# First layer of a diffusion block: modulation piece turned before the first inverse rms, which stays in PSUM

## The chip, the cores and the metric

The kernel runs on one core of a Trainium2 chip. The metric is the device time of one launch in microseconds (us), the median of three runs. TensorE (PE) multiplies, VectorE (DVE) and ScalarE (ACT) do elementwise work, GpSimd (POOL) and SyncE (SP) are used here for transfers and small work.

## The reference, cut to what matters

Two layers act on 512 latent and 256 context tokens of width 1024. Only the beginning of layer 0 is touched:

```
m = silu(cond) @ w_mod + b_mod                 # shift, scale, gate ... per condition (c and c_ctx)
h = rmsnorm(x, norm_mix) * (1 + scale) + shift # latent tokens with c, context tokens with c_ctx
p = h @ w_in                                   # 2560 columns, 20 tiles of 128
```

So the first product needs the inverse rms of every token, and for each 128 channels the shift and scale of those channels.

## The kernel before, in words

Activations lie transposed: eight tiles `x[k]` of 128 channels x 776 columns (512 latent tokens, 8 columns of gap, 256 context tokens). Every product runs as three fp32r matmuls (L185 low weight x high input, L186 high weight x low input, L187 high x high), since each number is split into a high part (an ACT cast) and a low part (a DVE subtraction), for weights in `weights` and `split` (L164 to L175). A matmul covers 512 latent or 256 context columns.

`start` (L424 to L458) computes, in the order of the code:

- the sum of squares `ss` (ACT squares, DVE adds);
- piece 0 of the modulation: `mod_piece` (L227) loads four quarters of 512 KB (tile `wmod`), multiplies them with `csil` (32 matmuls, seen as 64 rows each of matmul and weight load, L238) into an accumulator in the PSUM slot `ms`, copies it to SBUF (ACT, L243), transposes it on PE (L244), copies that (ACT, L246) and adds the bias (DVE, L247); `make_gain` (L278) then gives the gain for two of the eight channel tiles. Piece q serves channel tiles 2q and 2q+1;
- the inverse rms in `rstd` (L316): means on PE (L303), Newton steps on six numbers per partition (DVE), a diagonal `rd` (DVE, L325), and two matmuls with ones (L335) that spread it over all partitions into a PSUM slot; ACT copies it to the SBUF tile `r` (L444);
- high and low parts of the first three weight tiles of `w_in`;
- piece 1, then for each pair of channel tiles `mod_in` (L343): `xr = x * r` (DVE, L348), gain and shift (ACT L357 with DVE L358 for tiles 0 and 1, ACT L360 for the others), cast and low part; then the products of these two channel tiles with the three weight tiles into the slots `sl[0]` to `sl[2]`. Pieces 2 and 3 are traced right after the products of tiles 0 and 1.

After that `layer0_input` (L461) gates slots 0 and 1 (`glu`: ACT L573, DVE L582) and goes on with the fourth weight tile, which needs slot 0 again.

PSUM: there are four `slot` tiles of 128 x 1024 fp32. Slot `ms` holds the accumulator in columns 0:128 and the transposed piece in 768:896. The inverse rms goes to columns 0:512 and 520:776 of `sl[0]`.

Order: the framework takes instructions in the order in which the Python code traces them, finds what must wait for what in that order, and puts in the waits. Within this it fills each engine's queue by a simulated timeline, so independent instructions may be issued in another order than traced. `issue_after(i)` adds one edge: what the block traces on the engine of `i` is queued behind `i`. Nothing in it waits for another engine. Transfers of this stage all go through SP's queue, in traced order, 16 quarters of `wmod` with 14 buffers.

Of the kernel before, what the change touches and what calls it, by code (L numbers as in the profile page):

```python
# [12 lines left out]
F32 = mybir.dt.float32  # L13
BF16 = mybir.dt.bfloat16
F32R = mybir.dt.float32r
I32 = mybir.dt.int32
AF = mybir.ActivationFunctionType
ALU = mybir.AluOpType
PSUM = bass.MemoryType.PSUM

P = 128
DM = 1024
KT = DM // P
# [4 lines left out]
T = C0 + CTX  # L28
# [36 lines left out]
class Kern:  # L65
# [98 lines left out]
    def split(self, src, hi, lo):  # L164

        self.act_mark = self.nc.scalar.copy(hi, src)  # L166
        self.mark = self.nc.vector.tensor_tensor(lo, src, hi.bitcast(F32), op=ALU.subtract)  # L167

    def weights(self, dram, n=1024, into=None):
# [54 lines left out]
                    self.nc.tensor.matmul(s[:, lo:hi], wh, xl, start=False, stop=k == len(rhs) - 1)  # L224


    def mod_piece(self, l, lo, hi, at, dram, acc, tr, room):  # L227

        nc = self.nc
        for quarter in range(4):  # L230
            if quarter == 2:
                yield
            w = room(quarter)
            nc.sync.dma_start(w, dram[quarter])
            for kk in range(2):
                k = quarter * 2 + kk
                for j in range(4):
                    nc.tensor.matmul(  # L238
                        acc[32 * j:32 * j + 2, :], self.csil[:, k, :], w[:, kk, j * P:(j + 1) * P],
                        start=k == 0, stop=k == KT - 1,  # L240
                    )
        sb = self.tmp.tile([P, P], F32, name="modsb", tag="r", bufs=1)
        nc.scalar.copy(sb, acc)  # L243
        nc.tensor.transpose(tr, sb, self.ident)  # L244
        sb = self.tmp.tile([P, P], F32, name="modsb", tag="r", bufs=1)
        nc.scalar.copy(sb, tr)  # L246
        nc.vector.tensor_tensor(  # L247
            self.mod[:, l, lo:hi, :].rearrange("p (a b) c -> p a b c", a=2)[:, :, at:at + 2, :],
            sb.rearrange("p (a b c) -> p a b c", a=2, b=2)[:, :, :, 0:2],
            self.p("bmod")[:, l * 48 + lo:l * 48 + hi].rearrange("p (a b) -> p a b", a=2)[:, :, at:at + 2]  # L250
            .unsqueeze(3).broadcast_to([P, 2, 2, 2]), op=ALU.add)
        yield
# [60 lines left out]
            eng.tensor_tensor(y, t, y, op=ALU.mult)  # L313
        return y

    def rstd(self, ss, segs, ones2, slot, eng=None, pool=None, project=None):  # L316

        nc = self.nc
        chunks = [c for lo, hi in segs for c in range(lo, hi, P)]
        n = len(chunks)  # L320
        o = slot
        off = segs[0][0] - segs[0][0] % C0
        y = self.inverse(ss, chunks, ones2, o[:, segs[0][0] - off:segs[0][0] - off + 2 * n], eng or nc.gpsimd)
        d = (pool or self.tmp).tile([P, n, P], F32, name="rd", tag="rd", bufs=1)
        nc.vector.tensor_tensor(  # L325
            d, self.ident.unsqueeze(1).broadcast_to([P, n, P]), y.unsqueeze(2).broadcast_to([P, n, P]), op=ALU.mult
        )
        if project:
            with self.tc.issue_after(self.stats.ins):
                next(project)  # L330
        i = 0
        with self.tc.issue_after(self.product.ins) if project else nullcontext():
            for lo, hi in segs:
                m = (hi - lo) // P
                nc.tensor.matmul(  # L335
                    o[:, lo - off:hi - off], self.onesm, d[:, i:i + m, :].rearrange("p n c -> p (n c)"), start=True, stop=True)
                i += m
        return o[:, segs[0][0] - off:segs[-1][1] - off]
# [4 lines left out]
    def mod_in(self, h, k, r, n, l, shift, segs, raw=None):  # L343

        nc = self.nc
# [13 lines left out]
            else:  # L359
                nc.scalar.activation(t[:, s0:s1], xr[:, s0:s1], AF.Identity, scale=gain, bias=add)  # L360
        if k < 2:
            nc.vector.tensor_tensor(h[k][1][:, lo:hi], t[:, lo:hi], h[k][0][:, lo:hi].bitcast(F32), op=ALU.subtract)  # L362
        else:
            self.split(t[:, lo:hi], h[k][0][:, lo:hi], h[k][1][:, lo:hi])

# [58 lines left out]
    def start(self, ph):  # L424
# [5 lines left out]
            self.square_in(k, 0, T)  # L430
        sl = [self.slot() for _ in range(3)]
        ms = self.slot()
        nc.vector.memset(ms[:, 0:P], 0.0)

        def piece(q):
            room = lambda _: ph.tile([P, 2, 512], F32, name="wmod", tag="wmod", bufs=14)
            for _ in self.mod_piece(0, 0, 16, 2 * q, a["wm0"][q], ms[:, 0:P], ms[:, 768:768 + P], room):
                pass
            self.make_gain(0, 0, 1, self.p("nmix")[:, 0:8], 2 * q, 2 * q + 2)

        piece(0)
        rp = self.rstd(self.ss, segs, self.ones2, sl[0], eng=nc.vector, pool=ph)
        r = self.tmp.tile([P, T], F32, name="r", tag="ss", bufs=1)
        nc.scalar.copy(r, rp)  # L444
        room = [[ph.tile([P, DM], F32R, name=t) for t in ("whi0", "wlo0")], None, None]
        first = [self.weights(a["w_in"][m], into=room[m]) for m in range(3)]
        piece(1)
        h = self.new_h()
        for q in range(4):
            for k in (2 * q, 2 * q + 1):  # L450
                self.mod_in(h, k, r, 0, 0, 0, segs)
            for k in (2 * q, 2 * q + 1):
                for s, w in zip(sl, first):
                    self.wide_gemm(s, w, h, segs, [k])
            if q == 0:
                piece(2)
                piece(3)
        return h, sl  # L458


# [793 lines left out]
```

## Time and profile before

| what | value |
|---|---|
| median of 3 runs | 1461.02 us (1460.01 to 1461.03) |
| the profiled execution | 1462.82 us, its span 1461.0 us |
| busy: PE, PE weight loads, DVE, ACT, POOL | 97%, 85%, 74%, 44%, 12% of the span |
| granted TensorE clock over the span | 0.997 |
| HBM traffic | 172 GB/s over the span |

Busy shares are means over stages with different limits. [...] An fp32 matmul has two rows, an fp32r one has one. "Idle before" an instruction is named after what ended it.

### The profile page before, as it was taken

The numbers are of one execution on the slowest core, as the hardware profiler recorded it, in microseconds if no ns is written. First come the engines' busy times: TensorE is split into PE (matmuls) and PEld (weight loads), VectorE is DVE, ScalarE is ACT, GpSimd is POOL, SyncE is SP. The second block draws the span as 40 slices with busy tenths as digits, with TensorE's granted clock in tenths as the row PEclk, the third lists the DMA queues.
The fourth block names the chain that finished last, engine by engine and source line by source line (L and its number), as shares of the span: only waits on it lengthen the run. The fifth ranks groups of instructions, "written<-read, shape, count | busy, mean of one in ns | idle before, by whom it ended". The sixth has DMA issues, their size and how long they took to land.

```text
span 1461.0 us, 24131 instructions
## 1 busy us (share of the span) xinstructions
PE 1421.9 (97%) x9470; PEld 1249.1 (85%) x9470; DVE 1083.3 (74%) x1750; ACT 649.8 (44%) x1105; POOL 181.3 (12%) x427
## 2 busy tenths in 40 slices
PE   5999999999999999999999999999999999999997
PEld 3888888888888888888888878867799999999897
DVE  6699998689878557565534679787767977777676
ACT  5422224473223223123213365687765745545455
POOL 0000001112222212112212110243200000000000
PEclk9999999999999999999999999999999999999999
DMA  9325433036787767847725315264532444444441
GB/s 375 113 71 174 159 116 130 30 101 204 212 223 190 218 194 197 250 156 185 162 98 100 111 59 159 67 134 110 122 116 97 157 152 158 146 156 157 148 130 68
DMA packets 80546, 215.69 MB, mean 148 GB/s; under 512 B 10032, under 2 KB 10160, under 8 KB 80304
## 3 DMA queue, kind: packets, MB, share of 16 engines
q1 hardware_dynamic: 63408, 174.29, 36.1%
q0 software_dynamic: 17024, 39.86, 13.0%
q8 instruction: 74, 1.21, 0.3%
q14 instruction: 40, 0.33, 0.1%
HBM read 209.39 MB, written 41.94 MB: 172 GB/s over the span
## 4 chain that ended last, share of the span: by engine, by line
PE 82%; DVE 7%; DMA 5%; ACT 3%; issue 2%; POOL 1%; SPq 0%; DVEq 0%; ACTq 0%
PE slot L185 20%; PE slot L186 20%; PE slot L187 19%; DMA wraw<-in_w_down 3%; PE av L1091 2%; DVE wlo L167 2%; PE pt L1081 2%; PE s L1062 2%; PE av L185 2%; PE av L186 2%; PE av L187 1%; ACT whi L166 1%; PE slot L220 1%; PE slot L224 1%; PE slot L221 1%
## 5 line engine op out<-in xcount | busy, mean ns | idle before, releaser
L185 PE MATMUL slot<-h,wlo 128*128 128x256 f32 (+1 forms) x1152 | 382.5, 334 | 2.8 <-DVE ub L582 1.2
L186 PE MATMUL slot<-h,whi 128*128 128x256 f32 (+1 forms) x1152 | 382.5, 333 | 0.2 <-DVE h L362 0.2
L187 PE MATMUL slot<-h,whi 128*128 128x256 f32 (+1 forms) x1152 | 382.7, 332 | 0.0
L166 ACT CAST whi<-wraw 128x1024 fp32r<-128x1024 f32 (+2 forms) x249 | 219.9, 892 | 240.8 <-PE slot L187 88.1
L167 DVE TENSOR_TENSOR wlo<-wraw,whi 128x1024 fp32r<-128x1024 f32 (+2 forms) x249 | 254.4, 1027 | 72.2 <-ACT whi L166 71.5
L185 PEld LDWEIGHTS slot<-h,wlo 128*128 128x128 f32 x1152 | 216.5, 188 | 29.0 <-issue 2.0
L186 PEld LDWEIGHTS slot<-h,whi 128*128 128x128 f32 x1152 | 217.0, 188 | 23.1 <-DVE h L362 0.5
L187 PEld LDWEIGHTS slot<-h,whi 128*128 128x128 f32 x1152 | 217.0, 188 | 21.8
L382 DVE SCALAR_TENSOR_TENSOR cf<-slot,par,cf 128x775 f32<-128x775 f32 (+1 forms) x92 | 92.6, 1009 | 97.8 <-ACT cf L380 97.7
L185 PE MATMUL slot<-gh,wlo 128*128 128x512 f32 (+1 forms) x435 | 148.8, 344 | 2.1 <-ACT gh L166 1.1
L186 PE MATMUL slot<-gl,whi 128*128 128x512 f32 (+1 forms) x435 | 147.9, 341 | 0.0
L187 PE MATMUL slot<-gh,whi 128*128 128x512 f32 (+1 forms) x435 | 147.6, 340 | 0.0
L380 ACT ACTIVATE cf<-slot,par 128x776 f32<-128x776 f32 (+1 forms) x46 | 41.4, 901 | 192.8 <-PE slot L187 188.7
L590 DVE SCALAR_TENSOR_TENSOR cacc<-ub,par,cacc 128x783 f32<-128x783 f32 x120 | 118.4, 1035 | 0.3
L266 DVE CUSTOM_DVE_ANT_0 junk<-wmod,cb 128x1024 bf16<-128x1024 f32 x80 | 97.5, 1218 | 22.1 <-DMA wmod<-in_wmt 20.5
L372 DVE SCALAR_TENSOR_TENSOR x<-slot,mod,x 128x256 f32<-128x256 f32 (+1 forms) x139 | 80.9, 612 | 40.9 <-PE slot L187 40.4
L185 PEld LDWEIGHTS slot<-gh,wlo 128*128 128x128 f32 x435 | 81.4, 188 | 12.7 <-ACT gh L166 1.3
L187 PEld LDWEIGHTS slot<-gh,whi 128*128 128x128 f32 x435 | 81.8, 188 | 9.8
L186 PEld LDWEIGHTS slot<-gl,whi 128*128 128x128 f32 x435 | 81.9, 188 | 9.6 <-DVE mod L247 0.2
L1069 DVE CUSTOM_DVE_ANT_0 sm<-s,mask,nsink 128x640 f32<-128x640 f32 (+1 forms) x58 | 46.6, 819 | 13.9 <-PE pt L1081 10.7
L860 ACT ACTIVATE sgf<-cf 128x776 f32<-128x776 f32 (+1 forms) x44 | 32.6, 742 | 53.6 <-DVE cf L382 53.6
L1072 ACT ACTIVATE sm<-sm,nm 128x513 f32<-128x513 f32 (+1 forms) x64 | 50.0, 785 | 10.7 <-DVE nm L1069 7.1
(333 smaller groups left out, 2873.3 us busy)
## 6 DMA issues: line engine op xcount, KB each, us to landing
s<-in_w_up POOLq DMA_DIRECT2D x114, 256.0 KB, 5.5
wmod<-in_wmt SPq DMA_DIRECT2D x56, 512.0 KB, 4.6
wraw<-in_w_up SPq DMA_DIRECT2D x50, 512.0 KB, 4.2
wmod<-in_wm SPq DMA_DIRECT2D x40, 512.0 KB, 5.1
wraw<-in_w_up SPq DMA_DIRECT2D x57, 256.0 KB, 2.9
wraw<-in_w_down SPq DMA_DIRECT2D x48, 256.0 KB, 3.1
wraw<-in_w_in SPq DMA_DIRECT2D x20, 512.0 KB, 3.9
wraw<-in_w_down SPq DMA_DIRECT2D x32, 320.0 KB, 3.0
```

What stands on the lines that cost most here:

```text
L166: self.act_mark = self.nc.scalar.copy(hi, src)
L167: self.mark = self.nc.vector.tensor_tensor(lo, src, hi.bitcast(F32), op=ALU.subtract)
L185: mm(out, lo, xh, start=first, stop=False)
L186: mm(out, hi, xl, start=False, stop=False)
L187: self.product = mm(out, hi, xh, start=False, stop=last)
L266: nc.vector.tensor_tensor_reduce(junk, w, self.cb[:, c, :], 1.0, 0.0, ALU.mult, ALU.add, col)
L372: self.nc.vector.scalar_tensor_tensor(self.x[k][:, lo:hi], acc, self.mod[:, l, chunk * 8 + k, c:c + 1], self.x[k][:, lo:hi], op0=ALU.mult, ...
L380: nc.scalar.activation(acc[:, :n], u[:, :n], AF.Copy, scale=w[:, 1:2])
L382: nc.vector.scalar_tensor_tensor(acc[:, o], u[:, i], w[:, j:j + 1], acc[:, o], op0=ALU.mult, op1=ALU.add)
L590: self.tapped = nc.vector.scalar_tensor_tensor(acc, ub[:, t:t + CB_N], w[:, t:t + 1], acc, op0=ALU.mult, op1=ALU.add)
L1069: scored = nc.vector.tensor_tensor_reduce(sm[:, :n], s[:, SEQ - nl:SEQ + CTX], mk, -SCALE, nsink[:, hd:hd + 1], ALU.add, ALU.min, nm)
L1072: self.scored = scored, nc.scalar.activation(sm[:, :n + 1], sm[:, :n + 1], AF.Exp, scale=-1.0, bias=nm, accum_out=z)
```

## The change

- `split` gets a helper `low`, so that the low part of a weight can be traced apart from its high part; `mod_piece` gets an argument `after`, behind which its matmuls are queued, and keeps its transpose and last copy as `mod_turned` and `mod_copied`.
- Slot `ms` now holds everything: the means (columns 0:12), then the inverse rms in 0:512 and 520:776, and both the accumulator and the transposed piece in 896:1024. The copy to SBUF is gone; `xr` reads the inverse rms from `ms`.
- The two spreading matmuls are queued behind the transpose of piece 0.
- The high parts of weight tiles 1 and 2 are queued behind the last copy of piece 0, the low parts of tiles 0 and 1 behind `rd`; the low part of tile 2 is traced after channel tile 0's `mod_in`, and channel tile 1's DVE work is queued behind it.
- The products are traced channel tile by channel tile. The first half of piece 1 (two quarters) is traced ahead of the first `xr`, its second half behind the products of channel tile 0; piece 2 behind those of tile 1, piece 3 behind those of tile 3.

```
     def split(self, src, hi, lo):
         self.act_mark = self.nc.scalar.copy(hi, src)
+        self.low(src, hi, lo)
+
+    def low(self, src, hi, lo):
         self.mark = self.nc.vector.tensor_tensor(lo, src, hi.bitcast(F32), op=ALU.subtract)
...
-    def mod_piece(self, l, lo, hi, at, dram, acc, tr, room):
+    def mod_piece(self, l, lo, hi, at, dram, acc, tr, room, after=None):
...
+            with self.tc.issue_after(after.ins) if after else nullcontext():
+                for kk in range(2):
...
-        nc.tensor.transpose(tr, sb, self.ident)
+        self.mod_turned = nc.tensor.transpose(tr, sb, self.ident)
...
-        nc.scalar.copy(sb, tr)
+        self.mod_copied = nc.scalar.copy(sb, tr)
...
         if k < 2:
-            nc.vector.tensor_tensor(h[k][1][:, lo:hi], t[:, lo:hi], h[k][0][:, lo:hi].bitcast(F32), op=ALU.subtract)
+            self.low(t[:, lo:hi], h[k][0][:, lo:hi], h[k][1][:, lo:hi])
...
-        nc.vector.memset(ms[:, 0:P], 0.0)
-
-        def piece(q):
+        nc.vector.memset(ms[:, 896:1024], 0.0)
+
+        def piece(q, after=None):
             room = lambda _: ph.tile([P, 2, 512], F32, name="wmod", tag="wmod", bufs=14)
-            for _ in self.mod_piece(0, 0, 16, 2 * q, a["wm0"][q], ms[:, 0:P], ms[:, 768:768 + P], room):
-                pass
+            yield from self.mod_piece(0, 0, 16, 2 * q, a["wm0"][q], ms[:, 896:1024], ms[:, 896:1024], room, after)
             self.make_gain(0, 0, 1, self.p("nmix")[:, 0:8], 2 * q, 2 * q + 2)
-        piece(0)
-        rp = self.rstd(self.ss, segs, self.ones2, sl[0], eng=nc.vector, pool=ph)
-        r = self.tmp.tile([P, T], F32, name="r", tag="ss", bufs=1)
-        nc.scalar.copy(r, rp)
-        room = [[ph.tile([P, DM], F32R, name=t) for t in ("whi0", "wlo0")], None, None]
-        first = [self.weights(a["w_in"][m], into=room[m]) for m in range(3)]
-        piece(1)
+        chunks = [c for lo, hi in segs for c in range(lo, hi, P)]
+        y = self.inverse(self.ss, chunks, self.ones2, ms[:, 0:2 * len(chunks)], nc.vector)
+        for _ in piece(0, self.stats):
+            pass
+        d = ph.tile([P, len(chunks), P], F32, name="rd", tag="rd")
+        rd = nc.vector.tensor_tensor(
+            d, self.ident.unsqueeze(1).broadcast_to(d.shape), y.unsqueeze(2).broadcast_to(d.shape), op=ALU.mult)
+        with self.tc.issue_after(self.mod_turned.ins):
+            for lo, hi in segs:
+                i, j = lo // P, (hi - lo) // P
+                rs = nc.tensor.matmul(ms[:, lo:hi], self.onesm, d[:, i:i + j, :].rearrange("p n c -> p (n c)"), start=True, stop=True)
+        r = ms[:, 0:T]
+
+        first, raws = [], []
+        for m in range(3):
+            raws.append(self.wts.tile([P, 1024], F32, name="wraw", tag="wraw", bufs=3))
+            nc.sync.dma_start(raws[m], a["w_in"][m])
+            first.append([ph.tile([P, DM], F32R, name=t) for t in ("whi0", "wlo0")] if m == 0 else
+                         [self.wts.tile([P, 1024], F32R, name=t, tag=t, bufs=3) for t in ("whi", "wlo")])
+            with self.tc.issue_after((self.mod_copied if m else self.means).ins):
+                nc.scalar.copy(first[m][0], raws[m])
+        with self.tc.issue_after(rd.ins):
+            self.low(raws[0], *first[0])
+            self.low(raws[1], *first[1])
+        second = piece(1)
+        with self.tc.issue_after(rs.ins):
+            next(second)
         h = self.new_h()
         for q in range(4):
             for k in (2 * q, 2 * q + 1):
-                self.mod_in(h, k, r, 0, 0, 0, segs)
-            for k in (2 * q, 2 * q + 1):
+                with self.tc.issue_after(self.mark.ins) if k == 1 else nullcontext():
+                    self.mod_in(h, k, r, 0, 0, 0, segs)
+                if k == 0:
+                    with self.tc.issue_after(self.mark.ins):
+                        self.low(raws[2], *first[2])
                 for s, w in zip(sl, first):
                     self.wide_gemm(s, w, h, segs, [k])
-            if q == 0:
-                piece(2)
-                piece(3)
+                if k == 0:
+                    with self.tc.issue_after(self.product.ins):
+                        for _ in second:
+                            pass
+            if q < 2:
+                for _ in piece(q + 2, self.product):
+                    pass
```

## Rows read from the trace of the kernel before

**Rows 1.** The page: span, busy times, chain by engine.

```profile
span 1461.0 us, 24131 instructions
PE 1421.9 (97%) x9470; PEld 1249.1 (85%) x9470; DVE 1083.3 (74%) x1750; ACT 649.8 (44%) x1105; POOL 181.3 (12%) x427
...
PE 82%; DVE 7%; DMA 5%; ACT 3%; issue 2%; POOL 1%; SPq 0%; DVEq 0%; ACTq 0%
```

**Rows 2.** Engines by stretch: busy PE, PEld, DVE, ACT, POOL, clock, DMA.

```profile
20.00:30.00 10.00, 6.92 (x90) 3.81 (x79) 9.93 (x15) 6.24 (x11) 0.00 (x0) 1.00 1.03 408
30.00:40.00 10.00, 10.00 (x111) 8.42 (x110) 5.69 (x10) 5.99 (x12) 0.00 (x0) 1.00 1.00 397
57.00:110.00 53.00, 51.85 (x329) 45.52 (x327) 51.03 (x56) 16.27 (x19) 0.00 (x0) 1.00 0.22 70
```

**Rows 3.** Timeline to the first products: start, us, engine, line, operation.

```profile
16.90 3.59 PE L238 MATMUL slot<-wmod,csil 128*2 128x128 f32 x64
...
19.84 0.96 DVE L325 TENSOR_TENSOR rd<-ident,ry 128x768 f32<-128x768 f32 x1
...
20.94 1.82 PE L335 MATMUL slot<-rd,onesm 128*128 128x512 f32 x4 [0.45 <-ACT modsb L243]
...
22.80 0.81 ACT L444 COPY r<-slot 128x776 f32<-128x776 f32 x1
...
24.12 1.83 DVE L348 TENSOR_TENSOR xr<-x,r 128x776 f32<-128x776 f32 x2
24.42 0.33 PEld L238 LDWEIGHTS slot<-wmod,csil 128*2 128x2 f32 x16 [0.27 <-DMA wmod<-in_wm]
...
26.07 0.16 DVE L278 SCALAR_TENSOR_TENSOR gain<-mod,par 128x4 f32<-128x4 f32 x1
26.26 2.52 ACT L357 ACTIVATE h<-xr,mod,gain 128x512 fp32r<-128x512 f32 x4 [2.49 <-DVE gain L278]
...
27.13 0.97 PE L185 MATMUL slot<-h,wlo 128*128 128x512 f32 x3 [0.81 <-ACT h L357]
...
28.85 0.50 PE L186 MATMUL slot<-h,whi 128*128 128x512 f32 x1 [0.21 <-DVE h L362]
```

**Rows 4.** Timeline of the middle and end of the first three weight tiles.

```profile
34.74 1.93 PE L238 MATMUL slot<-wmod,csil 128*2 128x128 f32 x64
...
37.41 0.27 PE L244 MATMUL slot<-ident,modsb 128*128 128x128 f32 x1
...
37.71 0.27 ACT L246 COPY modsb<-slot 128x128 f32<-128x128 f32 x1 [0.46 <-PE slot L244]
...
48.59 0.39 PE L185 MATMUL slot<-h,wlo 128*128 128x512 f32 x1
...
51.73 0.86 PE L185 MATMUL slot<-h,wlo 128*128 128x512 f32 x3
...
57.89 0.28 PE L187 MATMUL slot<-h,whi 128*128 128x256 f32 x1
```

**Rows 5.** Waits of ACT, 930 to 1100 us: total, times, longest us.

```profile
ACT oh L166 <- DVE ol L167: 1.1, 2, 0.7
```

**Rows 6.** Waits of PE, 20 to 60 us.

```profile
PE slot L238 <- ACT modsb L246: 1.0, 1, 1.0
```

**Rows 7.** Groups by shape, 0 to 60 us: busy us, mean ns, idle before.

```profile
L348 DVE TENSOR_TENSOR xr<-x,r 128x776 f32<-128x776 f32 x8 | 7.6, 962 | 3.2 <-ACT ht L360 3.2
L167 DVE TENSOR_TENSOR wlo<-wraw,whi 128x1024 fp32r<-128x1024 f32 x5 | 5.9, 1219 | 0.0
L167 DVE TENSOR_TENSOR h<-ht,h 128x776 fp32r<-128x776 f32 x6 | 5.5, 960 | 3.3 <-ACT h L166 3.3
L166 ACT CAST h<-ht 128x776 fp32r<-128x776 f32 x6 | 4.7, 833 | 0.0
L243 ACT COPY modsb<-slot 128x128 f32<-128x128 f32 x4 | 1.0, 258 | 0.2 <-PE slot L238 0.2
```

**Rows 8.** Line 609: a DVE product of the same width with a PSUM operand.

```profile
L609 DVE TENSOR_TENSOR z<-slot,gc x4: 960/965/967, 118.8 to 204.6; 128x776 f32<-128x776 f32 x4
```

More of the change, by code (lines that the diff above doesn't have):

```diff
@@ L234, in mod_piece @@
             nc.sync.dma_start(w, dram[quarter])
[L235 to L241, printed above, removed]
+            with self.tc.issue_after(after.ins) if after else nullcontext():
+                for kk in range(2):
+                    k = quarter * 2 + kk
+                    for j in range(4):
+                        nc.tensor.matmul(
+                            acc[32 * j:32 * j + 2, :], self.csil[:, k, :], w[:, kk, j * P:(j + 1) * P],
+                            start=k == 0, stop=k == KT - 1,
+                        )
         sb = self.tmp.tile([P, P], F32, name="modsb", tag="r", bufs=1)
         nc.scalar.copy(sb, acc)
-        nc.tensor.transpose(tr, sb, self.ident)
+        self.mod_turned = nc.tensor.transpose(tr, sb, self.ident)
         sb = self.tmp.tile([P, P], F32, name="modsb", tag="r", bufs=1)
-        nc.scalar.copy(sb, tr)
+        self.mod_copied = nc.scalar.copy(sb, tr)
         nc.vector.tensor_tensor(
@@ L314, in inverse, with rstd @@
         return y
-    def rstd(self, ss, segs, ones2, slot, eng=None, pool=None, project=None):
+    def rstd(self, ss, segs, ones2, slot, eng=None, project=None):
         nc = self.nc
@@ L323, in rstd @@
         y = self.inverse(ss, chunks, ones2, o[:, segs[0][0] - off:segs[0][0] - off + 2 * n], eng or nc.gpsimd)
-        d = (pool or self.tmp).tile([P, n, P], F32, name="rd", tag="rd", bufs=1)
+        d = self.tmp.tile([P, n, P], F32, name="rd", tag="rd", bufs=1)
         nc.vector.tensor_tensor(
```

## The prediction, made before the changed kernel ran

> **What bounds the kernel now.** The page comes first: PE is busy for 97% of the span, and the chain of work that ended last runs over it for 82% [rows 1]. So a microsecond that PE loses without cover is a microsecond of the kernel. Next come the windows, because a share over the span hides a stage: from 20 to 30 us PE is busy 6.92 of 10 us with DVE at 9.93 and DMA at 1.03, while from 30 to 40 us PE is full [rows 2]. Only the stretch before about 29 us has room; behind it PE is the limit. From 57 to 110 us PE and DVE are both above 96% [rows 2], and DVE's work there hangs on the first gate, which needs the first three weight tiles complete. A shift of their end therefore shifts all that follows; I see nothing that would absorb it.
>
> The timeline then says what sets the start. Piece 0's matmuls run at 16.90, the diagonal ends at 20.80, the spreading matmuls take 1.82 us, ACT copies the inverse rms at 22.80 for 0.81 us, xr starts at 24.12, the gain comes only at 26.07, ACT starts h at 26.26, PE multiplies at 27.13 and goes on without a break from 28.85 [rows 3]. In the last stage, one channel tile with three weight tiles takes 51.73 - 48.59 = 3.14 us, and the last product of the eight starts at 57.89 and ends at 58.17 [rows 4].
>
> **The start, part by part.** The copy of 0.81 us goes. xr reads PSUM instead: a DVE product of the same width with a PSUM operand takes 965 ns against 962 [rows 7, 8], so nothing is paid for that. The transpose of piece 0 now stands ahead of the spreading matmuls. From its row and its neighbours (start 37.41, 0.27 us, copy at 37.71 [rows 4]) it puts them off by about 0.45 us, from 22.76 to 23.2 us. In return the gain is there at about 22.4 instead of 26.07 us. The DVE work beside it (low parts of tiles 0 and 1, 1.22 us each [rows 7]) ends at about 24 us and is covered by what follows.
>
> If xr only had to wait for the inverse rms, it would start at 23.3. But the first half of piece 1 is traced ahead of it, in columns of the same PSUM tile. Its second quarter does not land before 24.42, and its matmuls then take 0.6 us [rows 3]. So xr starts at about 25.1, a microsecond later than before, and ends at 26.06. ACT begins h at 26.1, PE follows 0.87 us later (26.26 to 27.13 [rows 3]), at 26.97. The low part of h needs both ACT halves (half of 2.52 us [rows 3]) and 0.96 us of DVE [rows 7]: steady products from 28.45 instead of 28.85. Gain: **0.4 us**. The order of the transfers in SP's queue is the same as before and costs nothing; they are all traced in the same sequence, and only the second half of piece 1 waits longer to be used.
>
> The low part of weight tile 2 (1.22 us) stands between channel tiles 0 and 1 on DVE. Two weight tiles of products (2.1 us) cover it; without them it would cost the 1.22. The third L185 can no longer run early: **+0.2**. The second half of piece 1 ran in idle PE time, now it stands between products: half of 1.93 us [rows 4], **+1.0**.
>
> **The pieces and the reads of r.** Here the change adds waits. The inverse rms (columns 0:512, 520:776) now shares its slot with the accumulator and the transposed piece (896:1024), and xr reads it eight times in between. Two rows tell what sharing a PSUM tile means. In attention, ACT's cast of one head's columns sat idle until DVE had read another head's columns of the same tile: 1.1 us in two cases [rows 5]; both only read. In this stage, PE's accumulation in columns 0:128 sat idle for 1.0 us until ACT had read columns 768:896 of that slot [rows 6]. So accesses of two engines to one PSUM tile wait for each other, in traced order, though their columns differ. Hence xr of channel tile 1 waits for piece 1 to its last copy, xr of tiles 2 and 3 for piece 2, xr of tiles 4 and 5 for piece 3. Each piece is queued behind the products before it, and the products behind it need that xr. PE has nothing else to do then: the fourth weight tile needs slot 0, which is still being filled.
>
> [...]
>
> What one hole costs, from the end of a piece's matmuls:
>
> - The tail: ACT copy 0.26 [rows 7], transpose 0.27 and last copy 0.27 with their gaps. From the transpose's start to the last copy's end it is 37.98 - 37.41 = 0.57 [rows 4]; with the first copy and two gaps 1.07 us. Then bias and gain on DVE, two steps of 0.16 with gaps, 0.4; then xr 1.0 [rows 7]. Together 2.5 us.
> - Piece 1, channel tile 1: PE can begin 0.87 after xr, at 3.35; the low part is ready at 2.5 + 1.3 + 0.1 + 0.96 = 4.85. Three products (0.7) fit in between. Net **4.2 us**.
> - Pieces 2 and 3, channel tiles 2 and 4: two pairs of ACT halves (2.52 [rows 3]), a cast of 0.83, a low part of 0.96 [rows 7] with gaps: 2.5 + 2.52 + 0.9 + 1.0 = 6.9, less the 0.7 of early products: **6.2 us each**. If ACT casts the first tile before it works on the second, 1.25 less. I take the longer one, as the second tile's xr is ready when ACT has finished the first two halves. Before, the matmuls of pieces 2 and 3 stood in the queue while these steps ran; about 0.5 us of holes remained, which go.
>
> Sum: -0.4 + 0.2 + 1.0 + 4.2 + 6.2 + 6.2 - 0.5 = **+16.9 us**; with the shorter order +14.4. The profiled execution took 1462.82 us with a span of 1461.0 [rows 1]; the median is 1461.02, so the 1.8 us around the span are left as they are and the sum is put on the median: **1478 us**. The upper bound of unknown costs: a cast of the fourth tile's weights in ACT's queue ahead of a tail (up to 1 us).
>
> **Rivals.**
>
> 1. PE slows down in the holes. After the idle beginning, the 64 rows of piece 0 took 3.59 us, those of piece 2 in the dense stretch 1.93 [rows 3, 4]: a difference of 1.66 us, though the granted clock reads 1.00 in the stretches shown [rows 2]. Once for each of the two long holes makes +3.3: 1481 us, up to 1485. For: such a hole leaves PE over 5 us with one transpose. Against: the shape of the beginning (14 us with nothing) is far from this. [...]
> 2. The reads of r are not held by the pieces, because the parts of the tile are followed column by column. Then xr starts at 23.3, first product at 25.1, steady from 26.6; the second half of piece 1 costs its 1.0 and the rest is as dense as before: 1.2 to 2.2 us faster, 1459.3 us. This is the case on the other side. It decides if xr of tile 1 starts before piece 1 is turned. For it speaks only that the copy, 0.81, and a late gain do lie on the path now [rows 3]; against it [rows 5, 6].
> 3. The wait is there but holds less: reads wait for a piece's matmuls and not for its tail (1.5 less per hole), and ACT casts the first tile early (1.25 less for two). 16.9 - 4.5 - 2.5 = 9.9: 1471 us, with parts of it 1464 to 1472.
>
> That the change doesn't do what it says is hardly possible: the orders that matter are forced by edges.
>
> **How the numbers follow.** A measurement of this kernel can tell about 0.2% (2.9 us) from no change. Forecast (1473 to 1480) 0.55, rival 1 (1480 to 1485) 0.18, rival 3 (1464 to 1473) 0.11, rival 2 (1458 to 1460) 0.14; 0.02 is left for anything else. The range from 1464 to 1485 takes in the forecast and rivals 1 and 3, 0.84. Slower by over 0.2%: 0.55 + 0.18 + 0.11 = 0.84 and a little of the rest, 0.85. Rival 2 stays within 2.9 us: 0.12 for the same, and 0.03 for faster, should it gain more than I see.
>
> **What the profile would show.** Right: ACT's copy of r is gone; the gain stands near 22.4 us; the first xr starts near 25 us behind the second quarter of piece 1; PE shows three holes, behind the second half of piece 1 and behind pieces 2 and 3, of about 3 and 6 us with only a transpose in them; xr's idle time is put down to ACT's copy L246; the eighth channel tile's products end near 75 us instead of 58.17. Rival 1: matmuls behind a hole last longer than the same ones later on. Wrong: xr of channel tile 1 starts while piece 1 is still being multiplied, PE stays full from 29 us, and the first tiles end before 58 us.

## The result, and the profile after the change

The changed kernel takes **1485.8 us** (median of 5 runs, 1485.14 to 1486.63) against 1461.02 before: 1.017 times as long (95% interval 1.0160 to 1.0181), **24.8 us slower**. The forecast was 1478.0 with a range from 1464 to 1485. The sign, the place and the chain of waits came as forecast; the time lies 7.8 us above the forecast and 0.8 us above the range.

The page of the changed kernel, the lines that answer to [rows 1]:

```profile
span 1484.9 us, 24129 instructions
PE 1432.0 (96%) x9470; PEld 1255.9 (85%) x9470; DVE 1084.0 (73%) x1750; ACT 649.5 (44%) x1104; POOL 180.3 (12%) x427
```

The span grew by 23.9 us while PE has the same 9470 instructions and 10.1 us more of busy time. So time was lost in two ways: 13.8 us without work, and 10.1 us in which the same work took longer (this includes the start and the few products inside the holes). The engines by stretch say where (columns as in [rows 2]: length, busy PE, PEld, DVE, ACT, POOL, granted clock, DMA share, GB/s):

```profile
30.00:40.00 10.00, 6.63 (x52) 4.99 (x52) 4.17 (x8) 2.53 (x5) 0.00 (x0) 0.83 0.99 395
40.00:50.00 10.00, 6.45 (x80) 5.31 (x80) 3.29 (x6) 2.46 (x6) 0.00 (x0) 0.83 0.45 166
50.00:60.00 10.00, 8.28 (x32) 7.09 (x33) 1.84 (x2) 2.41 (x4) 0.00 (x0) 0.66 0.00 0
60.00:70.00 10.00, 4.88 (x75) 3.71 (x74) 5.65 (x8) 5.31 (x10) 0.56 (x12) 0.87 0.01 2
70.00:80.00 10.00, 10.00 (x48) 8.79 (x47) 2.03 (x4) 4.47 (x7) 0.00 (x0) 0.78 0.00 0
```

Before, PE was full from 30 us at a granted clock of 1.00 [rows 2]. Now it is full in none of the four stretches up to 70 us, and its clock is granted at 0.66 to 0.87. In the last of the five PE is busy all the time, but at 0.78 of its full clock.

The timeline of the start (line numbers have moved: the sums are L307, pieces L242, first copy L247, turn L248, last copy L250, bias L251, gain L282, spreading L454, xr L352, gain and shift L361 to L364, products L188 to L190). "Turn" is the transpose of a piece. Here and below, rows between those shown are left out:

```profile
21.38 0.48 PE L248 MATMUL slot<-ident,modsb 128*128 128x128 f32 x1 [0.39 <-ACT modsb L247]
22.21 2.93 PE L454 MATMUL slot<-rd,onesm 128*128 128x512 f32 x4 [0.35 <-ACT modsb L250]
22.39 0.16 DVE L282 SCALAR_TENSOR_TENSOR gain<-mod,par 128x4 f32<-128x4 f32 x1
25.07 1.73 PE L242 MATMUL slot<-wmod,csil 128*2 128x128 f32 x32
26.88 0.96 DVE L352 TENSOR_TENSOR xr<-x,slot 128x776 f32<-128x776 f32 x1 [2.52 <-PE slot L242]
30.24 0.80 PE L189 MATMUL slot<-h,whi 128*128 128x512 f32 x1 [0.77 <-DVE h L170]
```

The gain is there at 22.39 instead of 26.07 us [rows 3], as meant. But xr, which needs nothing but x and the inverse rms, does not start when the inverse rms is there (the spreading ends at 25.14); it starts at 26.88, when the first half of piece 1 has been multiplied into other columns of the slot (25.07 and 1.73 end at 26.80). That is 1.74 of the 2.52 us for which DVE stands; the rest is the spreading itself. The steady products begin at 30.24 instead of 28.85.

The first hole, behind the second half of piece 1, which ends at 35.57 (34.52 and 1.05):

```profile
36.02 0.33 PE L248 MATMUL slot<-ident,modsb 128*128 128x128 f32 x1 [0.44 <-ACT modsb L247]
38.63 0.96 PE L188 MATMUL slot<-h,wlo 128*128 128x512 f32 x3 [2.28 <-ACT h L361]
40.13 0.79 PE L189 MATMUL slot<-h,whi 128*128 128x512 f32 x1 [0.54 <-DVE h L170]
```

The second hole, behind piece 2, from the same view (the one behind piece 3, 60.70 to 69.52 us, repeats it row by row):

```profile
44.32 1.93 PE L242 MATMUL slot<-wmod,csil 128*2 128x128 f32 x64
46.37 0.27 ACT L247 COPY modsb<-slot 128x128 f32<-128x128 f32 x1 [6.01 <-PE slot L242]
46.69 0.33 PE L248 MATMUL slot<-ident,modsb 128*128 128x128 f32 x1 [0.44 <-ACT modsb L247]
47.06 0.27 ACT L250 COPY modsb<-slot 128x128 f32<-128x128 f32 x1 [0.42 <-PE slot L248]
47.44 1.83 DVE L352 TENSOR_TENSOR xr<-x,slot 128x776 f32<-128x776 f32 x2
48.43 2.51 ACT L364 ACTIVATE ht<-xr,mod,gain 128x512 f32<-128x512 f32 x4 [1.11 <-DVE xr L352]
50.85 1.56 ACT L166 CAST h<-ht 128x776 fp32r<-128x776 f32 x2
51.70 1.84 DVE L170 TENSOR_TENSOR h<-ht,h 128x776 fp32r<-128x776 f32 x2 [2.36 <-ACT h L166]
51.73 1.65 PE L188 MATMUL slot<-h,wlo 128*128 128x512 f32 x3 [4.71 <-ACT h L166]
53.17 0.63 PE L189 MATMUL slot<-h,whi 128*128 128x512 f32 x1
...
58.17 0.39 PE L189 MATMUL slot<-h,whi 128*128 128x512 f32 x1
```

Read it downwards: piece, copy, turn, copy, xr, ht, cast, products, one after the other, over three engines (PE, ACT, DVE), each idle for the others. (`ht` is xr with gain and shift; its cast and its low part, L170, are the h of the products.) The products do not need the piece they wait for: piece q serves channel tiles 2q and 2q+1, and here tile 2 waits for piece 2 (in the other holes tile 1 for piece 1, tile 4 for piece 3). Between 46.25 and 51.73 us PE does one transpose. And the products behind it last 0.63 us each where the same kind last 0.39 us 5 us later. The waits of 14 to 90 us name the links of the chain (total us, times, longest):

```profile
PE slot L188 <- ACT h L166: 9.4, 2, 4.7
PE slot L188 <- ACT h L361: 4.2, 2, 2.3
DVE xr L352 <- PE slot L242: 2.5, 1, 2.5
```

In each hole the bias of the piece (L251; 47.35 us in the second) also stands just ahead of xr in DVE's queue, so these rows alone do not tell a held read from a place in DVE's queue. At tile 0 nothing stands between: xr follows piece 1's first half directly. E1 below takes away the sharing, and with it both.

Tile by tile this adds up. Holes, from the end of a piece's matmuls to the first steady product, less 0.7 us of early products: 40.13 - 35.57 - 0.7 = 3.9, 53.17 - 46.25 - 0.7 = 6.2, 69.52 - 62.63 - 0.7 = 6.2 us, together 16.3. Slower products: a tile's rest takes 4.2 to 4.5 us behind each hole where the same rest takes about 2.6 us at a granted clock of 1.00 (E4 below): +1.5, +1.7, +1.9, and +1.7 for tile 0; together 6.8. The second half of piece 1 among the products: 1.05. The start: 1.4. The sum is about 25.5; the first product of the fourth weight tile starts at 84.64 instead of 59.32 us, 25.3 later. Of this 1.4 us are given back later in the program (span +23.9).

### The profile page after: what moved, and what is told of

It reads as the page before. It is cut to its first block, busy times and chain, and to the rows that moved or that the text cites. A ratio compares the mean times of both kernels' runs of the same rounds, so it can differ in the third digit from the quotient of the medians.

```text
span 1484.9 us, 24129 instructions
## 1 busy us (share of the span) xinstructions
PE 1432.0 (96%) x9470; PEld 1255.9 (85%) x9470; DVE 1084.0 (73%) x1750; ACT 649.5 (44%) x1104; POOL 180.3 (12%) x427
## 4 chain that ended last, share of the span: by engine, by line
PE 82%; DVE 6%; DMA 5%; ACT 3%; issue 2%; POOL 1%; SPq 0%; DVEq 0%; ACTq 0%
PE slot L188 20%; PE slot L189 20%; PE slot L190 19%; PE av L1121 2%; PE pt L1111 2%; PE s L1092 2%; PE av L188 2%; PE av L189 2%; PE av L190 2%; DVE wlo L170 2%; DMA wraw<-in_w_down 2%; DMA wmod<-in_wm 2%; PE pt L188 1%; PE pt L189 1%; PE pt L190 1%
## 5 line engine op out<-in xcount | busy, mean ns | idle before, releaser
L188 PE MATMUL slot<-h,wlo 128*128 128x256 f32 (+1 forms) x1152 | 385.4, 337 | 15.5 <-ACT h L166 9.4
L190 PE MATMUL slot<-h,whi 128*128 128x256 f32 (+1 forms) x1152 | 385.7, 335 | 0.0
L166 ACT CAST whi<-wraw 128x1024 fp32r<-128x1024 f32 (+2 forms) x246 | 216.8, 890 | 235.2 <-PE slot L190 89.5
L170 DVE TENSOR_TENSOR wlo<-wraw,whi 128x1024 fp32r<-128x1024 f32 (+2 forms) x249 | 254.7, 1028 | 68.7 <-ACT whi L166 67.6
L188 PEld LDWEIGHTS slot<-h,wlo 128*128 128x128 f32 x1152 | 218.7, 190 | 42.7 <-ACT h L166 9.8
L189 PEld LDWEIGHTS slot<-h,whi 128*128 128x128 f32 x1152 | 219.6, 191 | 25.1 <-DVE h L170 2.4
L190 PEld LDWEIGHTS slot<-h,whi 128*128 128x128 f32 x1152 | 219.7, 191 | 21.9
L188 PE MATMUL slot<-gh,wlo 128*128 128x512 f32 (+1 forms) x435 | 148.8, 344 | 2.3 <-ACT gh L166 1.1
L190 PE MATMUL slot<-gh,whi 128*128 128x512 f32 (+1 forms) x435 | 147.6, 340 | 0.0
L188 PEld LDWEIGHTS slot<-gh,wlo 128*128 128x128 f32 x435 | 81.4, 188 | 12.9 <-ACT gh L166 1.3
L190 PEld LDWEIGHTS slot<-gh,whi 128*128 128x128 f32 x435 | 81.8, 188 | 9.8
```

The source lines that it names most:

```text
L188: mm(out, lo, xh, start=first, stop=False)
L189: mm(out, hi, xl, start=False, stop=False)
L190: self.product = mm(out, hi, xh, start=False, stop=last)
```

## The experiments

Twelve kernels, each timed beside runs of the kernel before on the same chip (1460.7 to 1461.1 us there). Ratios are to those, of means and not of medians. No run stands under the numbers E6 and E9.

| | what it is | us, median (range) | ratio (95%) |
|---|---|---|---|
| E1 | inverse rms copied to SBUF again | 1463.5 (1462.52 to 1467.57) | 1.0023 (1.0014 to 1.0032) |
| E2 | only its context columns copied | 1479.53 (1478.69 to 1481.37) | 1.0129 (1.0112 to 1.0146) |
| E3 | reads traced ahead of the pieces | 1475.18 (1472.26 to 1475.98) | 1.0093 (1.0078 to 1.0108) |
| E4 | holes filled with idle products | 1478.47 (1477.56 to 1480.23) | 1.0120 (1.0105 to 1.0135) |
| E5 | half of piece 1 not queued behind tile 0 | 1480.86 (1479.94 to 1481.92) | 1.0138 (1.0124 to 1.0152) |
| E7 | E1, pieces 2 and 3 together | 1462.64 (1460.95 to 1465.54) | 1.0015 (1.0006 to 1.0024) |
| E8 | E7, half of piece 1 free | 1462.62 (1461.19 to 1464.9) | 1.0013 (1.0004 to 1.0022) |
| E10 | only piece 0 early, copy kept | 1462.34 (1461.51 to 1463.64) | 1.0011 (1.0002 to 1.0020) |
| E11 | before, TensorE busy ahead of the sums | 1462.87 (1460.85 to 1463.4) | 1.0010 (1.0001 to 1.0019) |
| E12 | E10, the same | 1461.7 (1461.25 to 1463.54) | 1.0007 (0.9998 to 1.0016) |
| E13 | before, a shorter filling | 1461.26 (1460.0 to 1464.57) | 1.0008 (0.9999 to 1.0017) |
| E14 | E7, the shorter filling | 1468.56 (1465.42 to 1469.35) | 1.0050 (1.0038 to 1.0063) |

### E1: the shared slot taken away

```diff
-        r = ms[:, 0:T]
+        r = self.tmp.tile([P, T], F32, name="r", tag="ss", bufs=1)
+        nc.scalar.copy(r, ms[:, 0:T])
```

> The changed kernel with one thing undone: ACT copies the inverse rms from the slot to SBUF, and xr reads the copy; every queued order of the change stays. Theory (the reads of the shared slot wait for the pieces, and PE idles and slows down behind them): the three holes go, the products of the first three weight tiles are dense again, their last one ends at 57 to 61 us instead of 83.7, and the time is 1459 to 1464 us. Rival (the forced places of the pieces between the products are what costs, sharing or not): the holes stay in part, the last product ends behind 70 us, and the time is above 1470 us.

1463.5 us: one copy of 0.81 us on ACT takes back 22.3 of the 24.8 us. The timeline and two stretches of E1:

```profile
22.18 1.56 PE L454 MATMUL slot<-rd,onesm 128*128 128x512 f32 x4 [0.35 <-ACT modsb L250]
24.76 0.97 DVE L352 TENSOR_TENSOR xr<-x,r 128x776 f32<-128x776 f32 x1 [0.43 <-ACT r L456]
28.12 0.50 PE L189 MATMUL slot<-h,whi 128*128 128x512 f32 x1 [0.76 <-DVE h L170]
```

```profile
30.00:40.00 10.00, 10.00 (x135) 7.93 (x134) 7.76 (x14) 6.68 (x13) 0.00 (x0) 1.00 1.02 404
40.00:50.00 10.00, 10.00 (x112) 8.61 (x112) 4.89 (x5) 4.79 (x8) 0.56 (x12) 1.00 0.46 170
```

xr now starts right behind the copy (24.76 us), beside piece 1's first half (24.78) and not behind it; the three holes are gone (one wait of 1.4 us for h stays, at 54.10), the clock is granted at 1.00. All the rest of the change (the early turn, the edges, the moved low part) was left as it is and costs 2.4 us. So the loss hangs on the eight xr reading the slot that the pieces also use.

### E2: how much of a slot is guarded

```diff
-        r = ms[:, 0:T]
+        rc = self.tmp.tile([P, T], F32, name="r", tag="ss", bufs=1)
+        nc.scalar.copy(rc[:, SEQ:T], ms[:, SEQ:T])
+        r = [(0, SEQ, ms[:, 0:SEQ]), (SEQ, T, rc[:, SEQ:T])]
```

with xr made in two parts, the latent one (columns 0:512) still from PSUM.

> The changed kernel with only the context part of the inverse rms (columns 512 to 776) copied to SBUF; the latent part (0 to 512) is still read from the slot that the pieces use in columns 896 to 1024. If the slot's two halves of 512 columns are kept apart, each by itself: no read meets a piece, the holes go, 1459 to 1464 us. If the whole slot tile is guarded, as the 1.0 us wait of PE in the kernel before let it seem: the holes stay as in the changed kernel, 1484 to 1489 us.

1479.53 us, between what the theories gave, so the time alone does not decide; the timeline does. The pieces write columns 896:1024 only, in the other half of the slot:

```profile
24.43 0.43 DVE L353 TENSOR_TENSOR xr<-x,r 128x264 f32<-128x264 f32 x1
24.45 1.05 PE L242 MATMUL slot<-wmod,csil 128*2 128x128 f32 x32 [0.61 <-ACT r L457]
25.57 0.69 DVE L353 TENSOR_TENSOR xr<-x,slot 128x512 f32<-128x512 f32 x1 [0.26 <-PE slot L242]
```

The context part starts on time, the latent part only when piece 1's first half has ended (25.50); for tile 1 it starts at 34.85, behind the last copy of piece 1 (34.47 and 0.27) and behind the bias that needs this copy, so the clean case is tile 0. DVE had stood for 0.26 us there and started 0.07 us after the piece. So the whole slot is guarded, not the half that is touched, as [rows 6] had it for two engines in two halves. The median is 6.3 us below the changed kernel. By the profiles the fourth weight tile starts 7.5 us earlier (77.13 instead of 84.64): 2.1 at the start, 0.7 in the first hole, 3.0 in the two long ones (the waits of PE for h are 3.4 instead of 4.7 us, as a part of the context work is done ahead), and 1.6 because tile 1's products take 0.39 us for 512 columns instead of 0.63 (together 2.64 instead of 4.19 us).

### E3: reads ahead of the pieces in traced order

```diff
+                    xrs[1] = self.scaled(1, r, 0, T)
                     with self.tc.issue_after(self.product.ins):
                         for _ in second:
...
             if q < 2:
+                for k in (2 * q + 2, 2 * q + 3):
+                    xrs[k] = self.scaled(k, r, 0, T)
                 for _ in piece(q + 2, self.product):
```

> The changed kernel with the slot still shared, but xr of channel tile 1 traced ahead of the second half of piece 1, xr of tiles 2 and 3 ahead of piece 2, xr of tiles 4 and 5 ahead of piece 3. Theory (each read waits for the pieces traced ahead of it, so the order of tracing makes the holes): PE has the activation steps of the next tile beside the pieces, no hole over 2 us is left behind a piece, 1459 to 1465 us. Rival (sharing costs in any order, since pieces then wait for the reads): 1472 us or more.

1475.18 us, on the rival's side and a miss for my theory that the traced order alone makes the holes; but it takes back 10.6 of the 24.8 us, so the order carries a part. The timeline of E3 (the fastest of its four runs, 1472.26 us) shows what stays:

```profile
38.60 0.27 PE L248 MATMUL slot<-ident,modsb 128*128 128x128 f32 x1
38.91 0.27 ACT L250 COPY modsb<-slot 128x128 f32<-128x128 f32 x1 [2.65 <-PE slot L248]
39.30 1.83 DVE L349 TENSOR_TENSOR xr<-x,slot 128x776 f32<-128x776 f32 x2
41.23 3.57 PE L242 MATMUL slot<-wmod,csil 128*2 128x128 f32 x64 [2.35 <-ACT whi L166]
```

The read of tiles 2 and 3 is now ahead of piece 2, but it is still behind piece 1, whose turn stands in PE's queue behind tile 1's products (38.60; its input was there at 36.27). Then piece 2 waits for the read: 39.30 and 1.83 end at 41.13, and PE had stood for 2.35 us (the row names ACT's cast, but that ended at 40.36). So pieces wait for reads as reads wait for pieces. A second wait, 2.97 us ahead of 62.83, follows piece 3's turn, which also stands behind products (56.91); tile 6 does need that piece.

### E4: the holes kept, TensorE kept at work in them

```diff
+        def fill(n):
+            with self.tc.issue_after(self.mod_turned.ins):
+                for _ in range(n):
+                    nc.tensor.matmul(sl[0][:, 776:1024], first[0][0][:, 0:P], first[0][0][:, P:P + 248], ...)
```

called with 16 behind piece 1 and 36 behind pieces 2 and 3 (and one clearing of these columns on DVE at the very start); the columns are used by nothing else.

> The changed kernel with matmuls that compute nothing needed (16 behind piece 1's transpose, 36 behind those of pieces 2 and 3, 248 columns each, into columns that nobody reads) in the holes, so that PE is not idle there; they take less than the holes. Theory (of the excess over the forecast, most is PE slowed down after each hole, seen as 0.63 us instead of 0.39 for 512 columns): products behind pieces 1, 2 and 3 take 0.39 us, 5 to 8 us less than the changed kernel: 1478 to 1481 us. Rival (the slow matmuls have another cause, for instance the reading of weights or transfers at that time): 1484 to 1488 us.

1478.47 us, 7.3 less than the changed kernel, with more work on PE. Its timeline and stretches:

```profile
43.72 4.38 PE L477 MATMUL slot<-whi 128*128 128x248 f32 x36
49.08 0.96 PE L188 MATMUL slot<-h,wlo 128*128 128x512 f32 x3 [0.98 <-ACT h L166]
...
64.42 0.50 PE L189 MATMUL slot<-h,whi 128*128 128x512 f32 x1 [0.19 <-DVE h L170]
```

```profile
50.00:60.00 10.00, 9.57 (x114) 8.38 (x114) 2.04 (x5) 0.56 (x3) 0.56 (x12) 1.00 0.01 2
60.00:70.00 10.00, 9.21 (x60) 7.89 (x59) 6.55 (x9) 9.24 (x13) 0.00 (x0) 1.00 0.01 2
```

The wait for h is no shorter (5.12 us from the end of the turn at 43.96 to the products, 4.71 in the changed kernel), but the clock stays at 1.00 and the products run at full speed at once (0.39 us for 512 columns from the second one on). So a part of the loss is not the wait but the lower clock behind it, 0.66 from 50 to 60 us in the changed kernel and 1.00 here. By the profiles, E4 gains 1.65 us at the start, where but for the clearing it is the same program, so not by the filling (see the last section), and 5.5 us behind the three pieces, 5.2 of it in products at full speed: the next weight tile's first product is at 77.48 instead of 84.64. Tile 0's products, ahead of which nothing is filled, stay slow in E4 (0.63 us from 28.59 on); in E1, where xr does not wait for piece 1, they last 0.39 us.

### E5: one of the three holes taken away

```diff
-                    with self.tc.issue_after(self.product.ins):
-                        for _ in second:
-                            pass
+                    for _ in second:
+                        pass
```

> The changed kernel with one ordering edge taken away: the second half of piece 1 is no longer queued behind tile 0's products. Theory (every hole is one serial chain piece, turn, xr, h, products, and the products behind it run at the lower clock): the first of the three holes goes, 3.9 us, and with it the slower products of tile 1, 1.7 us, so 1485.8 - 5.6 = 1480.2 us (1478.5 to 1482.5); the two long holes of 6.2 us stay. Rival (the chain only moves to where the half now stands, between tile 0's products): 1484.5 us or more.

1480.86 us, 4.9 less than the changed kernel where 5.6 was expected: the theory's side. xr of tile 1 now starts at 31.23 instead of 36.77, PE waits for h ahead of tile 1 for 1.2 instead of 2.3 us, and tile 1's products run at full speed (34.59 to 37.23, 2.64 us, at a granted clock of 1.00 from 30 to 40 us); the two long waits stay (9.7 us together). A part of the 4.9 us can be the start: the spreading took 1.56 us in E5's profile and 2.93 in the changed kernel's (see the last section).

### E7, E8, E10: what the rest of the change is worth without the shared slot

E7 is E1 with pieces 2 and 3 together again, as before; E8 is E7 with E5's edit.

```diff
-            if q < 2:
-                for _ in piece(q + 2, self.product):
-                    pass
+            if q == 0:
+                for p in (2, 3):
+                    for _ in piece(p, self.product):
+                        pass
```

> E1 (inverse rms copied to SBUF) with pieces 2 and 3 both behind tile 1's products again, as in the kernel before, instead of one behind tile 1 and one behind tile 3. Theory (what E1 still loses is the 1.4 us in which tile 4's products wait for ACT's h, because piece 3 is turned only at 49.8 us): that wait goes and the time falls from 1463.5 to 1462.0 us (1461.2 to 1462.8). Rival (E1's remaining 2.4 us is the second half of piece 1 among the products and work later in the program): 1463.2 us or more.

> The kernel of the run ahead, and in it the second half of piece 1 no longer queued behind tile 0's products either. Theory (the half, 1.05 us, then runs in the gap in which TensorE waits for h ahead of tile 0's whi products): another 1.0 us less, 1461.0 us (1460.2 to 1462.0), level with the kernel before. Rival (the half's last quarter lands after the gap and stops the products behind it on TensorE): 1462.5 us or more.

E7: 1462.64 us, inside what was expected. The 1.4 us wait of E1 is gone; the 0.9 us between the medians lies within the two intervals. E8: 1462.62, a miss: nothing more. In E8's trace TensorE stands for 0.70 us among tile 1's products instead, for the low part of h, and not for the late quarter that the rival named.

E10 takes E1 and puts what stands behind piece 0 back into the order of before: pieces whole, the edges in the loop over channel tiles gone, both tiles of a pair modulated ahead of their products. The edges on the weights' high and low parts stay.

```diff
-                    with self.tc.issue_after(self.mark.ins):
-                        self.low(raws[2], *first[2])
+        self.low(raws[2], *first[2])
+        for _ in piece(1):
+            pass
...
+            if q == 0:
+                for p in (2, 3):
+                    for _ in piece(p):
+                        pass
```

> One part of the change alone: piece 0 turned ahead of the inverse rms (which is copied to SBUF as before); pieces 1 to 3 and the low parts of the weights in the order of the kernel before. Theory (the turned piece lies beside VectorE's inverse, so gain is there at 22.4 instead of 26.07 us and the first products start earlier by 0.7 us, all else as before): 1460.3 us (1459.3 to 1461.2). Rival (the low parts of the weights and tile 1's xr, which now stand ahead of tile 0's h on VectorE, put the start back by 1 us or more): 1462 us or more.

1462.34 us: the rival. Its timeline:

```profile
22.25 1.56 PE L454 MATMUL slot<-rd,onesm 128*128 128x512 f32 x4 [0.36 <-ACT modsb L250]
22.43 0.16 DVE L282 SCALAR_TENSOR_TENSOR gain<-mod,par 128x4 f32<-128x4 f32 x1
23.17 2.36 DVE L170 TENSOR_TENSOR wlo<-wraw,whi 128x1024 fp32r<-128x1024 f32 x2 [0.58 <-ACT whi L465]
25.45 1.83 DVE L352 TENSOR_TENSOR xr<-x,r 128x776 f32<-128x776 f32 x2
```

Turning piece 0 first puts the spreading off from 20.94 to 22.25 us [rows 3], and the low parts, themselves late by 0.58 us behind the high parts that are queued behind piece 0, stand ahead of the two xr (25.45 instead of 24.12). Tile 0's xr is ready at about 26.4, no earlier than the late gain of before (26.07), DVE's part of h starts at 27.20 instead of 26.27, and the first steady product at 29.78 instead of 28.85. The gain was late, but with it early the next step waits for xr. In this form the idea of the change gains nothing; E10 does not test it without the edges on the weights.

### E11 to E14: an attempt at a version faster than both

The sums ahead of the inverse rms take 2.72 us and piece 0 3.59 us at the start, where a piece takes 1.93 later. E11 and E12 put 14 products of 256 columns on the arriving x ahead of the sums, E13 and E14 put 9:

```diff
+        for k, n in enumerate((1, 1, 1, 1, 2, 2, 2, 4)):
+            for _ in range(n):
+                nc.tensor.matmul(sl[1][:, 0:256], self.onesm, self.x[k][:, 0:256], start=True, stop=True)
```

> The kernel before, with 14 idle-filling products of 256 columns on the arriving x ahead of the sums of squares (into a slot that is still free), so that TensorE has worked when the sums come at 14.25 us. Theory (after its first 14 us without work TensorE runs at the lower clock until about 21 us: twelve sums in 2.72 us, 64 products of piece 0 in 3.59 us where later pieces take 1.93 us): the sums take about 1.4 us less and with them the inverse rms and the first products come earlier; 1460.7 - 1.2 = 1459.5 us (1458.8 to 1460.3). Rival (the first products wait for the weights' low parts and for piece 1's transfers instead): 1460.4 us or more.

> The same filling in the kernel with piece 0 turned ahead of the inverse rms and the copy to SBUF kept (E10, 1462.3 us). Theory (sums 1.4 us and piece 0 1.6 us shorter, so that the turned piece no longer holds back the spreading of the inverse rms, 22.25 us against 20.94 before): 1462.3 - 2.2 = 1460.1 us (1459.0 to 1461.3). Rival (tile 1's xr and the low parts of the weights still stand ahead of tile 0 on VectorE, and the time stays): 1461.8 us or more.

> The kernel before with 9 instead of 14 filling products ahead of the sums, so that the filling ends before 14.3 us (in E11 it ended at 15.98 and put the sums back by 1.6 us, though they took 1.40 instead of 2.72 us). Theory: the sums start on time and the inverse rms comes 1.2 us earlier; what of it reaches the first products depends on VectorE's third low part and gain, 26.1 us before: 1460.0 us (1459.3 to 1460.6). Rival (piece 1's transfers, for which TensorE waited 2.6 us in E11, set the start): 1460.8 us or more.

> E7 (piece 0 turned ahead, second half of piece 1 behind tile 0's products, inverse rms copied to SBUF, pieces 2 and 3 together) with the same 9 filling products. Theory (sums 1.3 us and piece 0 1.6 us shorter; tile 0's products no longer stand behind a transfer of piece 1, so the first whi product comes at about 26 us instead of 28.85; 1.05 us of piece 1 come back among the products): 1459.2 us (1458.2 to 1460.3), below both kernels. Rival (the second or third w_in row or its low part is late instead): 1461 us or more.

The timeline of E11 shows shorter sums and a shorter piece, as the theory had them. That the clock made the difference it does not show: from 14 to 20 us the column reads 1.00 here and before. The result is still a miss:

```profile
15.82 1.40 PE L303 MATMUL slot<-ones,ss 128*128 128x2 f32 x12
17.15 1.93 PE L238 MATMUL slot<-wmod,csil 128*2 128x128 f32 x64
```

Sums and piece take 1.40 and 1.93 us instead of 2.72 and 3.59, about half, but the filling ended late and put the sums back by 1.6 us: 1462.87, the rival's side. In E13 the sums start on time (14.49) and take 1.50 us; then the spreading takes 2.90 us again, the gain comes at 26.71, behind the third low part, and the first steady product at 29.49: 1461.26, the rival's side, and no measurable difference to before. E12 (1461.7, the theory's upper end was 1461.3) has its gain at 20.80 and then starts its steady products at 28.79: piece 1's last quarter comes late (27.91 to 28.53), and the wait that ends last is that for h's low part (28.74), which stands on DVE behind tile 1's xr and the third weight's low part, as the rival had it. E14 has the earliest start of all, 26.83 instead of 28.85 us, and is slow, a plain miss:

```profile
34.60 0.27 PE L248 MATMUL slot<-ident,modsb 128*128 128x128 f32 x1
...
35.41 0.17 DVE L282 SCALAR_TENSOR_TENSOR gain<-mod,par 128x4 f32<-128x4 f32 x1
...
38.90 0.96 PE L188 MATMUL slot<-h,wlo 128*128 128x512 f32 x3 [1.75 <-ACT h L166]
```

Piece 1's turn (its first copy ended at 31.15) is issued behind tile 1's products, so tile 2 waits, PE is busy for 1.15 and 1.07 us of the two stretches of 2 us from 36 to 40 us, and from 40 to 44 us its clock is granted at 0.54 and 0.61. The changed kernel's kind of loss comes again here, made by an order in PE's queue and not by a shared slot. One profile shows it, that of the fastest of five runs; the rest of the 7.8 us is not traced. No version here beats the kernel before.

## Where the prediction was right, and the step that failed

- **That reads and pieces wait for each other in one slot**, inferred from [rows 5, 6]: right. E1 takes the sharing away and with it 22.3 us; E2 shows that it holds across the slot's halves. The second rival (reads not held), the faster side, did not happen: xr started 1.74 us after the inverse rms was there, behind piece 1.
- **The size of the holes**, 4.2, 6.2 and 6.2 us: measured 3.9, 6.2 and 6.2. That the long ones agree so closely is in part luck: the low part was ready about 6.4 us behind the piece (52.7), not 6.9, and the three early products took 1.44 us (51.73 to 53.17) where 0.7 was counted. The longer order on ACT (both tiles' halves before the casts) was the right choice. The third rival (shorter holds) falls with it.
- **The start**, -0.4 us: measured +1.4 in the profiled execution, in which the spreading took 2.93 us. In E4, the same program up to there with the spreading at 1.56, xr starts at 25.22 (forecast 25.1) and the steady products at 28.59 (28.45). The working was right for an execution in which the spreading takes 1.56 us, and did not ask whether it does. This term was 1.8 us too low for the profiled execution.
- **The second half of piece 1**, +1.0: 1.05. **The third early product**, +0.2, is too small to be seen by itself. **The 0.5 us of old holes that go** has no row: from 28.85 to 58.17 us PE of the kernel before is busy for 29.32 of 29.32 us, so the term should have been nothing.
- **That nothing absorbs the shift**: nearly, 1.4 of 25.3 us.
- **The step that failed is the first rival, "PE slows down in the holes"**, which I priced at 1.66 us for each of the two long holes and set beside the forecast with a chance of 0.18; in the sum it stood at nothing. It was not a rival but a term: it came behind all three holes and over tile 0 too, and cost 1.5 to 1.9 us a time, 6.8 us in all. Even with the rival's 3.3 us the forecast is 1481. The price of one was near, though taken from other work (piece 0). The argument against it ("the shape of the beginning, 14 us with nothing, is far from this") was wrong: behind the first hole, from 35.57 to 40.13 us, with one transpose and three products in it, the products were slow as well (0.63 us for 512 columns from 40.72 on, the clock granted at 0.67 from 38.60 to 43.20). E4 shows it: with PE at work in the same waits, the products behind them run at full speed, 5.2 us by the profiles (7.3 us between the medians, the start included). 16.9 of forecast with these 6.8 and 1.8 at the start make 25.5 us. Products of 512 columns start 0.43 us apart behind a hole (53.17 to 53.60) and 0.22 us apart later (58.17 to 58.39; their rows, 0.63 and 0.39 us long, overlap). The clock is granted at 0.50 from 53.17 to 57.00 us and at 1.00 from 58.17 to 60.60.
- **A reading:** "the granted clock reads 1.00 in the stretches shown [rows 2]" was set beside piece 0, but those stretches begin at 20 us, behind it (16.90 to 20.49). The stretch from 14 to 20 us reads 1.00 too, which is the subject of the last section.
- **The signs:** the eighth channel tile's products ended at 83.72 us, not near 75. The wait of DVE in the holes is put down to ACT's last copy, as written, but on the row of the bias (21.2 us in three waits), which stands ahead of xr.

What stays open: the rest of E14's loss, and what sets TensorE's pace at the start (last section).

## What to carry to other kernels

A result that is read many times does not belong into a PSUM tile into which other work is still written: here the waits followed the tile, not its columns (in E2 a read of columns 0:512 started 0.07 us after a piece in 896:1024 had ended), and a copy of 0.81 us was worth 22.3 us. When a change opens holes of a few microseconds on TensorE, add to each hole the slower work behind it as a term of the sum; here that was 1.5 to 1.9 us behind holes that cost 4 to 6 us. And before something is moved ahead because it is late, ask what the next step waits for: the gain came 3.7 us earlier and the steady products 1.4 us later.

## What the hardware showed that was not expected

**TensorE's pace at the start differs between executions of the same instructions.** E1 and E7 issue the same instructions to TensorE up to channel tile 2's first products. The spreading and the first half of piece 1 in E7's profile, beside 1.56 and 1.05 us in E1's:

```profile
22.16 2.93 PE L454 MATMUL slot<-rd,onesm 128*128 128x512 f32 x4 [0.35 <-ACT modsb L250]
25.98 1.89 PE L242 MATMUL slot<-wmod,csil 128*2 128x128 f32 x32 [0.90 <-ACT r L456]
```

E7's steady products then start at 29.33 instead of 28.12 us. That execution took 1465.54 us, the longest of 11; E1's 1463.17, near its median. The changed kernel's profiled execution began like E7's (2.93 us) and was the longest of its five, E4's like E1's (1.56 us). Of the nine profiles of the changed kernel and its variants without filling ahead of the sums, six (E1 to E5, E10) have the spreading at 1.56 us and three (the changed kernel, E7, E8) at 2.93. What decides it is not shown. Differences of 1 to 2 us between two profiles can come from this alone.

**The granted clock of a stretch does not show it**: from 20 to 30 us the changed kernel's row reads 1.00, as E1's does, though the spreading took 2.93 us in the one and 1.56 us in the other. In E13, where it took 2.90 us, the column reads 0.83. That TensorE was slow there is read from the durations, which nearly double for the same instructions; that a low clock was the reason is my inference, and the column of the changed kernel does not show it. At the start I go by a known instruction's duration, not by the column.
